# Writing the turned blocks of 16 of the 32 groups of up rows from ScalarE's DMA queue instead of SyncE's, in a two-layer decoder trunk

## The chip, the cores and the metric

The kernel runs on one core of a Trainium2 chip. The metric is the device time of one launch in microseconds (us). Three runs of the kernel before took 2085.42, 2086.52 and 2086.86 us; their median is 2086.52 us.

## What is computed

Two decoder layers on 256 tokens of width 2048, all in float32. Layer 0 mixes tokens with forgetting attention (16 heads of 128), layer 1 with a mixture of three dilated windows (8 heads). Each mixer and each MLP adds to the residual stream `x`. The change touches the MLPs alone:

```python
def sq_relu_mlp(h, w_up, w_down):
    a = jax.nn.relu(h @ w_up)
    return (a * a) @ w_down

def reference(...):
    for i in range(DEPTH):
        ...
        h = rms_norm(x, mlp_norm_g[i])
        x = x + sq_relu_mlp(h, mlp_w_up[i], mlp_w_down[i]).astype(x.dtype)
    return x
```

Here `w_up` is 2048 x 8192 and `w_down` 8192 x 2048, in each of the two layers.

## The kernel before, in words

**Products.** TensorE multiplies in a rounded 32-bit format, so every weight block is cut in two: ScalarE casts it to `hi` (L403) and VectorE subtracts that from the loaded block to give `lo` (L409). Three products (hi by hi, lo by hi, hi by lo) make one exact enough product. A weight block is 256 rows of 512 columns; SyncE loads it into one of seven `raw` buffers (L396), to which each MLP adds one more (`mlp_raw`). There are four `hi` and four `lo` buffers, and each MLP adds one `hi` (`mlp_hi`). A block in the plain form takes twelve matmuls of 512 columns (L456 to L458). In the "halved" form (`parts`, with the L471 matmuls) VectorE first makes sums of quarters of the block (L490, L495, L497), in a second `raw` buffer, and TensorE then needs 21 matmuls of 256 columns, about seven eighths of the plain work, from two pairs of `hi` and `lo`.

**The MLP.** It runs in four periods of 2048 hidden columns. Period b makes four groups of up rows of 512 columns each ("ups"). From the second period on they run mixed with the four "downs" of the period before, block by block, in the order that a table of letters U and D gives. What an up gives is needed by the downs of the next period.

**The end of an up** (`up_end`, L1214). ScalarE reads the banks and applies the relu (L1232) into `z`; VectorE transposes `z` in squares of 32 by 32 into `turned` (L1235, the tile `mlp_tr`, three buffers); four DMAs write `turned` to a buffer in DRAM so that the squares come to stand in order (`moved_blocks`, L570, the tile `blocks`, four buffers; each DMA moves 128 KB); one DMA of 512 KB reads it back into `z` (L575); ScalarE squares it (L1243) and copies it to `aT` (L1248), the stationary operand of the downs.

**The order.** All work is first recorded as operations with an engine, an assumed duration, and what they read and write (`add`). `Plan.order` then runs a list schedule over the engines PE, ACT, DVE, POOL and one "dma" line that stands for SyncE's queue, with due times worked back from the products, and the program is emitted in the order of the planned starts. So each engine, and SyncE's queue, has one fixed order; an instruction whose semaphore has not come holds up everything behind it on its engine. SyncE issues the weight loads, the block writes and the read-backs in that one order.

**Names in the rows.** `raw`, `mlp_raw`: loaded weights. `hi`, `mlp_hi`, `lo`: the cuts. `mlp_z` and `mlp_sums`: rooms for rows ahead of the transposition. `blocks`: the DRAM buffer.

Of the kernel before, what the change touches and what calls it, by code (L numbers as in the profile page):

```python
# [20 lines left out]
NT = S // P  # L21
NC = 512
# [13 lines left out]
PERIODS = DFF // D  # L36
# [12 lines left out]
LAST_HALVED = [[[], [], [4, 5, 6, 7], []], [[], [6, 7], [4, 5, 6, 7]]]  # L49
# [9 lines left out]
ROWS_BY_DMA = {"fox": (), "dil": ()}  # L59
UP_BY_DMA = [[(), (0, 1, 2, 3), (), ()], [(), (0, 1, 2, 3), (), ()]]  # L60
SHARED = 2
N_W = {"fox": 4, "dil": 3}
TURNED = {"fox": "DDDE", "dil": "DDDE"}
ROUNDS = 4
# [9 lines left out]
EARLY_NORM = 0.0  # L74
EARLY_HEADS = 0.0
EARLY_ROWS = 0.0
# [191 lines left out]
def trunk(ctx: ExitStack, tc, x, fox_w_in, fox_b_f, fox_q_gain, fox_k_gain, fox_w_out, dil_w_in,  # L268
          dil_q_gain, dil_k_gain, dil_w_out, mix_norm_g, mlp_norm_g, mlp_w_up, mlp_w_down, out):
    nc = tc.nc  # L270
    plan = Plan(["fox", "mlp0", "dil", "mlp1"])
    add = plan.add
    T = {}

    def v(item):
        return T[item.slot if isinstance(item, Item) else item]
# [35 lines left out]
    for ph in ("mlp0", "mlp1"):  # L312
        rings[ph] = dict(sigma=ring("sigma", 4, 2 * 4 * 2 * P, ph), tr=ring("tr", N_TR, NT * NC, ph),
                         z=ring("z", N_Z, 4 * S, ph), c=ring("c", N_C, 4 * S, ph), sums=ring("sums", 1, NT * NC, ph))
# [247 lines left out]
        return [[(room, x) for x in names] for names in (("12", "11"), ("22", "21"))]  # L562


    def moved_blocks(turned, into, early=0.0):

        blocks = blocks_ring.take()
        for i in range(4):
            def go(i=i):
                nc.sync.dma_start(v(blocks)[:, :, i, :].rearrange("j c y -> c j y"),  # L570
                                  v(turned)[32 * i:32 * i + 32, 0:NT * NC].rearrange("c (j y) -> c j y", j=4))
            add("dma", 0.4, go, reads=[turned], writes=[(blocks, i)])

        def back():
            nc.sync.dma_start(v(into)[:, 0:NT * NC], v(blocks).rearrange("j c i y -> (j c) (i y)"))  # L575
        add("dma", moved(512), back, reads=[(blocks, i) for i in range(4)], writes=[into], early=early)
        return [into]
# [22 lines left out]
    def normed(l, n, col, phase, source, sigmas):  # L600

        own = rings[phase]
        turned, back = (own["w"].take(), own["w"].take()) if phase == "fox" else (own["tr"].take(), own["z"].take())
        add("dve", 1.4, lambda: nc.vector.transpose(
            v(turned).rearrange("p (j t b r) -> p t b j r", t=NT, j=4, b=4),
            v(f"x{n}").rearrange("p (t b j c) -> p t b j c", t=NT, j=4, c=32)), reads=x_keys(n), writes=[turned])
        here = moved_blocks(turned, back, EARLY_NORM)
# [331 lines left out]
    for n in range(NX):  # L939
# [5 lines left out]
        for pr in range(2):  # L945
# [12 lines left out]
            for i in range(2):  # L958
                b = 2 * pr + i
# [27 lines left out]
        reads=[wf, (wfs, 0)], writes=[(wfs, 1)])  # L987
# [223 lines left out]
    out_proj(oT, fox_w_out[0], then1, "fox", sigma_o)  # L1211


    def up_end(l, phase, source, halved, by_dma, room, summed=None, rows_by_dma=False):  # L1214
        own = rings[phase]

        def end(banks):
# [7 lines left out]
            else:  # L1225
                c = own["c"].take()
# [9 lines left out]
                v(turned).rearrange("p (j t b r) -> p t b j r", t=NT, j=4, b=4),  # L1236
                v(z)[:, 0:2 * NC].rearrange("p (t b j c) -> p t b j c", t=NT, j=4, c=32)),
                reads=[(z, t) for t in range(NT)], writes=[turned, z])
            here = moved_blocks(turned, z, EARLY_ROWS)

            for t in range(NT):
                def squared(t=t):
# [21 lines left out]
    def mlp(l, layer, phase, source, sigmas, then, last=None):  # L1264
        more_weights(phase, MORE)
        downs = []
        turn = 0
        for b in range(PERIODS):
            a, a_sums = Source(), {}
            ups = []  # L1270

            def sum_of(n):
                a_sums[n] = rings[phase]["sigma"].take()
                return a_sums[n]
            for n in range(4):
                halved = HALVED[layer][b][n]
                banks = (AC if halved else AC[:2]) if b or n % 2 == 0 else BE if halved else BE[:2]
                ups.append(Unit(source, mlp_w_up[layer], 0, [(b * D + n * NC, NC)], banks,
                                up_end(l, phase, a, halved, LOW_BY_DMA and n < 3, "z" if b or n % 2 == 0 else "sums",
                                       (lambda n=n: sum_of(n)) if b == PERIODS - 1 and any(j // 2 == n for x in LAST_HALVED[layer] for j in x) else None, n in UP_BY_DMA[layer][b]),  # L1280
                                halved, sigmas, UP_ADDING[layer][b][n]))
            if b == 0:
                paired(ups[0], ups[1])
                ups[2].blocks(NP)
                ups[3].blocks(NP)
            else:
                for u, d in zip(ups, downs):
                    for c in UU_D[layer][b - 1]:
                        (u if c == "U" else d).block()
            downs = []  # L1290
            for n in range(NX):
                banks = ("E0", "E1") if turn % 2 == 0 else ("B0", "B1")
                turn += 1
                here = LAST_HALVED[layer][n] if b == PERIODS - 1 and n < len(LAST_HALVED[layer]) else ()
                if b == PERIODS - 1:
                    banks = rows_of_banks(LAST_BANKS[layer][n])
                end = quarters_to_x(n, then, here, rings[phase]["c"]) if here else add_to_x(n, then) if b == PERIODS - 1 else add_to_x(n, None, rings[phase]["sums"] if BY_DMA else None)
                downs.append(Unit(a, mlp_w_down[layer], b * D, [(n * NC, NC)], banks, end, here, a_sums, ADDING if b < PERIODS - 1 else ()))
        if last is None:
            paired(downs[0], downs[1])  # L1300
            downs[2].blocks(NP)
            downs[3].blocks(NP)
        else:
            paired(downs[0], downs[1])
            downs[2].blocks(NP)
            last(downs[3])
        fewer_weights(phase)
# [207 lines left out]
```

## Time and profile before

| what | value |
|---|---|
| median of 3 runs | 2086.52 us (2085.42 to 2086.86) |
| the profiled execution | 2085.53 us |
| its span, from the first to the last instruction | 2083.7 us |
| PE busy | 2078.4 us, 12118 matmuls |
| VectorE (DVE) busy | 1882.1 us |
| ScalarE (ACT) busy | 1472.0 us |
| GpSimd (POOL) busy | 116.1 us |
| granted TensorE clock | 1.000 |
| bytes moved by DMA | 528.57 MB, mean 254 GB/s |

How to read it: the span lies 1.8 us under the time of its own execution, and that execution is one run among those of the first row. Busy times are unions of an engine's instructions. The instructions that issue a DMA, or wait for a semaphore, are not counted as busy, so ScalarE's 1472.0 us hold none of the work that this change gives to it. In the rows of the timeline the columns are the start in us from the span's start, the duration in us, engine, line, operation, what is written and read, shapes and count; in brackets stands how long the engine was idle just before and what ended that.

### The profile page before, as it was taken

To read this page: it belongs to the slowest core of one execution; us is meant where nothing else is said; L and a number is where in the kernel's file an instruction comes from. 1 tells how busy PE (TensorE), PEld (TensorE's weight loads), DVE (VectorE), ACT (ScalarE), POOL (GpSimd) and SP (SyncE) were. 2 spreads that over 40 slices of the span, in tenths; PEclk is the share of its full clock that TensorE was granted. 3 is DMA by queue.
4 is the path that set the end of the run, shared out by engine and by line. 5 is a ranking of instruction groups with operands and counts; after the bars stand their busy time and mean duration, and the time that the engine had idled before them with its cause. 6 is when DMAs were issued, how large, how long until landed. Compare 5 with 4: busy or idle time off the path is not lost.

```text
span 2083.7 us, 33916 instructions
## 1 busy us (share of the span) xinstructions
PE 2078.4 (100%) x12118; PEld 1889.3 (91%) x12118; DVE 1882.1 (90%) x2612; ACT 1472.0 (71%) x2151; POOL 116.1 (6%) x115
## 2 busy tenths in 40 slices
PE   9999999999999999999999999999999999999999
PEld 8899888899999999998888999888999999999988
DVE  8999899999989999988799999777999999999987
ACT  7778767677677676776677777656776777676664
POOL 1100100000010000000010000100000000000000
PEclk9999999999999999999999999999999999999999
DMA  8688968698897798797877778868798888897894
GB/s 277 204 243 259 279 197 265 222 290 277 242 302 253 252 273 260 251 294 249 268 232 247 234 218 271 255 203 265 238 284 259 263 278 247 272 281 227 254 301 159
DMA packets 341467, 528.57 MB, mean 254 GB/s; under 512 B 52072, under 2 KB 145072, under 8 KB 341296
## 3 DMA queue, kind: packets, MB, share of 16 engines
q1 hardware_dynamic: 330784, 497.94, 72.7%
q0 software_dynamic: 10240, 28.32, 7.5%
q8 instruction: 95, 1.56, 0.3%
q14 instruction: 76, 0.62, 0.1%
q10 hardware_dynamic: 272, 0.13, 0.0%
HBM read 458.80 MB, written 39.19 MB: 239 GB/s over the span
## 4 chain that ended last, share of the span: by engine, by line
PE 100%; POOL 0%; DVE 0%; issue 0%; POOLq 0%
PE bank_C L471 14%; PE bank_A L471 14%; PE bank_B L456 11%; PE bank_B L458 11%; PE bank_B L457 11%; PE bank_E L471 10%; PE bank_E L456 6%; PE bank_E L457 6%; PE bank_E L458 6%; PE bank_A L456 3%; PE bank_A L458 3%; PE bank_A L457 3%; PE bank_C L847 1%; PE bank_C L892 1%; PE bank_C L845 0%; PE bank_B L471 0%
## 5 line engine op out<-in xcount | busy, mean ns | idle before, releaser
L403 ACT CAST hi<-raw 128x1024 fp32r<-128x1024 f32 (+2 forms) x808 | 802.1, 1003 | 406.2 <-PE bank_B L458 112.6
L409 DVE TENSOR_TENSOR lo<-raw,hi 128x1024 fp32r<-128x1024 f32 (+2 forms) x808 | 925.5, 1161 | 113.0 <-ACT hi L403 67.4
L457 PE MATMUL bank_B<-lo,aT 128*128 128x512 f32 x576 | 218.3, 379 | 0.0
L471 PE MATMUL bank_C<-hi,hT 128*128 128x256 f32 (+1 forms) x782 | 207.2, 302 | 0.0
L456 PE MATMUL bank_B<-hi,aT 128*128 128x512 f32 x500 | 189.7, 379 | 0.0
L458 PE MATMUL bank_B<-hi,aT 128*128 128x512 f32 x500 | 189.5, 379 | 0.0
L457 PE MATMUL bank_E<-lo,aT 128*128 128x512 f32 x480 | 181.9, 379 | 0.0
L471 PE MATMUL bank_A<-hi,mlp_sigma 128*128 128x256 f32 x880 | 171.6, 275 | 0.0
L457 PE MATMUL bank_B<-lo,hT 128*128 128x512 f32 x448 | 169.8, 379 | 0.0
L456 PE MATMUL bank_B<-hi,hT 128*128 128x512 f32 x436 | 166.3, 381 | 0.0
L458 PE MATMUL bank_B<-hi,hT 128*128 128x512 f32 x436 | 165.2, 379 | 0.0
L403 ACT CAST mlp_hi<-raw 128x1024 fp32r<-128x1024 f32 (+1 forms) x123 | 122.3, 995 | 58.1 <-PE bank_E L458 22.0
L471 PE MATMUL bank_E<-hi,hT 128*128 128x512 f32 (+1 forms) x556 | 163.0, 355 | 0.0
L471 PEld LDWEIGHTS bank_C<-hi,hT 128*128 128x128 f32 x782 | 148.1, 191 | 4.5
L409 DVE TENSOR_TENSOR lo<-raw,mlp_hi 128x1024 fp32r<-128x1024 f32 (+1 forms) x123 | 141.4, 1150 | 10.6 <-issue 2.4
L471 PE MATMUL bank_C<-lo,hT 128*128 128x256 f32 (+1 forms) x495 | 150.7, 305 | 0.0
L471 PEld LDWEIGHTS bank_A<-hi,mlp_sigma 128*128 128x128 f32 x880 | 145.5, 192 | 0.0
L471 PE MATMUL bank_A<-lo,mlp_sigma 128*128 128x256 f32 x521 | 143.3, 275 | 0.0
L456 PE MATMUL bank_E<-hi,aT 128*128 128x512 f32 x356 | 135.0, 379 | 0.0
L458 PE MATMUL bank_E<-hi,aT 128*128 128x512 f32 x356 | 134.9, 379 | 0.0
L490 DVE TENSOR_TENSOR raw<-raw 128x512 f32<-128x512 f32 x172 | 116.9, 684 | 10.3 <-DMA raw<-in_mlp_w_up_dram 10.2
L457 PEld LDWEIGHTS bank_B<-lo,aT 128*128 128x128 f32 x576 | 109.0, 189 | 14.0
(453 smaller groups left out, 4896.3 us busy)
## 6 DMA issues: line engine op xcount, KB each, us to landing
raw<-in_mlp_w_down_dram SPq DMA_DIRECT2D x224, 512.0 KB, 5.7
raw<-in_mlp_w_up_dram SPq DMA_DIRECT2D x223, 512.0 KB, 5.5
raw<-in_dil_w_in_dram SPq DMA_DIRECT2D x192, 256.0 KB, 4.5
raw<-in_fox_w_in_dram SPq DMA_DIRECT2D x94, 512.0 KB, 5.2
blocks<-mlp_tr SPq DMA_DIRECT2D x176, 128.0 KB, 4.2
mlp_z<-blocks SPq DMA_DIRECT2D x40, 512.0 KB, 6.2
mlp_raw<-in_mlp_w_up_dram SPq DMA_DIRECT2D x33, 512.0 KB, 5.5
raw<-in_fox_w_out_dram SPq DMA_DIRECT2D x32, 512.0 KB, 4.3
```

The lines of the kernel that those rows point to most:

```text
L403: add("act", on_act(n), lambda: nc.scalar.copy(r(hi)[:, 0:n], v(src)[:, at:at + n]), reads=keys, writes=[hi])
L409: add("dve", on_dve(n), lambda: nc.vector.tensor_sub(r(lo)[:, 0:n], v(src)[:, at:at + n], v(hi)[:, 0:n]), reads=[*keys, hi], writes=[lo])
L456: nc.tensor.matmul(acc, a, h, start=first and i == 0, stop=False)
L457: nc.tensor.matmul(acc, a, l, start=False, stop=False)
L458: nc.tensor.matmul(acc, b, h, start=False, stop=last and i == 1)
L471: nc.tensor.matmul(to if part is None else to[:, part * S:(part + 1) * S], stationary, moving, start=first, stop=last)
L490: add("dve", on_dve(2 * q), lambda: nc.vector.tensor_add(v(sums)[:, 0:2 * q].rearrange("p (g n) -> p g n", g=2), v(raw)[:, q:3 * q].rearra ...
L847: nc.tensor.matmul(ps[:, P:3 * P], r(a)[:, own], in_turn(r(b)[:, both], P // 2), start=opens and x == 0, stop=x == 2)
L892: nc.tensor.matmul(acc[:, 0:S], r(w)[:, c:c + P], in_turn(r(q), P), start=first, stop=False)
```

## The change

A table `UP_BY_ACT` names ups by layer, period and number. It names all four ups of the second and the third period of both MLPs, 16 of the 32. For these the four block writes leave SyncE's order: ScalarE issues them, one behind the other, as a single operation of the plan, which reads `turned` and so follows the transposition. In the plan it takes 4 x 0.43 us of ScalarE's time, and a second operation without an instruction stands for the transfer. A second table for the norms, `NORM_BY_ACT`, is empty. The read-backs stay on SyncE. Nothing is computed otherwise.

```diff
+UP_BY_ACT = [[(), (0, 1, 2, 3), (0, 1, 2, 3), ()]] * 2
+NORM_BY_ACT = ()
...
-    def moved_blocks(turned, into, early=0.0):
+    def moved_blocks(turned, into, early=0.0, by_act=False):
         blocks = blocks_ring.take()
-        for i in range(4):
+        if by_act:
+            def there():
+                for i in range(4):
+                    nc.scalar.dma_start(v(blocks)[:, :, i, :].rearrange("j c y -> c j y"),
+                                        v(turned)[32 * i:32 * i + 32, 0:NT * NC].rearrange("c (j y) -> c j y", j=4))
+            all_four = [(blocks, i) for i in range(4)]
+            add("act", 4 * Plan.ISSUE, there, reads=[turned, *all_four])
+            add("dma", 1.6, None, reads=[turned], writes=all_four).soon = 0.8
+        for i in () if by_act else range(4):
             def go(i=i):
                 nc.sync.dma_start(v(blocks)[:, :, i, :].rearrange("j c y -> c j y"),
...
-            here = moved_blocks(turned, z, EARLY_ROWS)
+            here = moved_blocks(turned, z, EARLY_ROWS, turned_by_act)
```

The plan is made anew from the changed operations. PE's order and GpSimd's come out row for row as they were. On ScalarE, VectorE and SyncE the order differs in places. In the rows below the lines of the change are two higher than before up to L567 and ten higher from there on (L403 is L405, L570 is L580 or, for ScalarE, L573).

ScalarE in the second period of the first MLP, at the end of its first up, before (this is the stretch from 490 to 499 us of the profile):

```order
L1232 ACTIVATE mlp0_z0_3077<-mlp0_z0_3077,rstd1_75 128x512
L403 CAST hi1_128<-raw4_124 128x768
L403 CAST hi2_129<-raw5_125 128x1024
L403 CAST hi3_130<-raw6_126 128x1024
L403 CAST mlp0_hi0_3081<-raw0_120 128x768
L403 CAST hi0_127<-raw1_121 128x1024
```

The same place with the change:

```order
L1242 ACTIVATE mlp0_z0_3077<-mlp0_z0_3077,rstd1_75 128x512
L405 CAST hi1_128<-raw4_124 128x768
L405 CAST hi2_129<-raw5_125 128x1024
L573 DMA blocks0_143<-mlp0_tr2_3076 32x4x256 x4
L405 CAST hi3_130<-raw6_126 128x1024
L405 CAST mlp0_hi0_3081<-raw0_120 128x768
L405 CAST hi0_127<-raw1_121 128x1024
```

The four DMAs stand behind the second cast that follows the relu, and five casts of weights stand right behind them.

SyncE at the same end of an up, before:

```order
L570 DMA blocks0_143<-mlp0_tr2_3076 32x4x256 x4
L396 DMA raw4_124<-in_mlp_w_down_dram 128x2x512
L396 DMA raw5_125<-in_mlp_w_up_dram 128x2x512
L396 DMA raw0_120<-in_mlp_w_up_dram 128x2x512
L575 DMA mlp0_z0_3077<-blocks0_143 128x1024
L396 DMA mlp0_raw0_3080<-in_mlp_w_down_dram 128x2x512
```

With the change:

```order
L398 DMA raw4_124<-in_mlp_w_down_dram 128x2x512
L398 DMA raw5_125<-in_mlp_w_up_dram 128x2x512
L398 DMA raw0_120<-in_mlp_w_up_dram 128x2x512
L585 DMA mlp0_z0_3077<-blocks0_143 128x1024
L398 DMA mlp0_raw0_3080<-in_mlp_w_down_dram 128x2x512
L398 DMA raw2_122<-in_mlp_w_down_dram 128x2x512
```

The block writes are gone, and the read-back stands behind the same three loads as before.

VectorE at the end of the last up of the second period of the second MLP, before (from 1688 to 1696 us):

```order
L409 TENSOR_TENSOR lo2_133<-raw0_120,hi0_127 128x1024
L409 TENSOR_TENSOR lo3_134<-raw1_121,mlp1_hi0_12317 128x1024
L490 TENSOR_TENSOR raw4_124<-raw3_123 128x512
L409 TENSOR_TENSOR lo0_131<-raw2_122,hi1_128 128x1024
L495 TENSOR_TENSOR raw4_124<-raw4_124,raw3_123 128x256
L1235 STREAM_TRANSPOSE mlp1_tr2_12312<-mlp1_z0_12313 128x8x4x32
```

With the change:

```order
L411 TENSOR_TENSOR lo2_133<-raw0_120,hi0_127 128x1024
L1245 STREAM_TRANSPOSE mlp1_tr2_12312<-mlp1_z0_12313 128x8x4x32
L411 TENSOR_TENSOR lo3_134<-raw1_121,mlp1_hi0_12317 128x1024
L411 TENSOR_TENSOR lo0_131<-raw2_122,hi1_128 128x1024
L492 TENSOR_TENSOR raw4_124<-raw3_123 128x512
L411 TENSOR_TENSOR lo1_132<-raw3_123,hi2_129 128x768
```

The transposition has moved ahead of two cuts and two sums, to right behind the cut that it followed at a distance.

More of the change, by code (lines that the diff above doesn't have):

```diff
@@ L606, in normed @@
             v(f"x{n}").rearrange("p (t b j c) -> p t b j c", t=NT, j=4, c=32)), reads=x_keys(n), writes=[turned])
-        here = moved_blocks(turned, back, EARLY_NORM)
+        here = moved_blocks(turned, back, EARLY_NORM, l in NORM_BY_ACT)
         for b in range(4):
@@ L1211, in trunk, with up_end @@
     out_proj(oT, fox_w_out[0], then1, "fox", sigma_o)
-    def up_end(l, phase, source, halved, by_dma, room, summed=None, rows_by_dma=False):
+    def up_end(l, phase, source, halved, by_dma, room, summed=None, rows_by_dma=False, turned_by_act=False):
         own = rings[phase]
@@ L1279, in mlp @@
                                 up_end(l, phase, a, halved, LOW_BY_DMA and n < 3, "z" if b or n % 2 == 0 else "sums",
-                                       (lambda n=n: sum_of(n)) if b == PERIODS - 1 and any(j // 2 == n for x in LAST_HALVED[layer] for j in x) else None, n in UP_BY_DMA[layer][b]),
+                                       (lambda n=n: sum_of(n)) if b == PERIODS - 1 and any(j // 2 == n for x in LAST_HALVED[layer] for j in x) else None, n in UP_BY_DMA[layer][b], n in UP_BY_ACT[layer][b]),
                                 halved, sigmas, UP_ADDING[layer][b][n]))
```

## The prediction, made before the changed kernel was run

> **What bounds the kernel now.** I read the page's busy times and its chain first, then the waits of PE, then PE's own rows, and last the four stretches in which the change acts.
>
> ```profile
> PE 2078.4 (100%) x12118; PEld 1889.3 (91%) x12118; DVE 1882.1 (90%) x2612; ACT 1472.0 (71%) x2151; POOL 116.1 (6%) x115
> ...
> PE 100%; POOL 0%; DVE 0%; issue 0%; POOLq 0%
> ```
>
> The chain that ended last is PE alone. A busy PE need not be a PE at its rate, since the ends of matmuls are modelled. So the next two views look for waits and at the distance from start to start.
>
> ```profile
> PE bank_C L908 <- POOL ident masks.py:199: 1.7, 1, 1.7
> ```
>
> That is the whole list of PE's waits (over 0.15 us): one, of 1.7 us, at the start of the program.
>
> ```profile
> 1734.24 0.38 PE L456 MATMUL bank_B<-hi,aT 128*128 128x512 f32 x1
> 1734.45 0.38 PE L457 MATMUL bank_B<-lo,aT 128*128 128x512 f32 x1
> 1734.67 0.38 PE L458 MATMUL bank_B<-hi,aT 128*128 128x512 f32 x1
> ```
>
> Matmuls of 512 columns start 0.21 to 0.22 us apart although each is drawn 0.38 long: they run one behind the other. The changed places lie in four stretches, the second and third period of each MLP (columns: length, busy time and count of PE, weight loads, DVE, ACT, POOL, then granted clock, DMA share, GB/s):
>
> ```profile
> 455.00:620.00 165.00, 165.00 (x1052) 152.72 (x1051) 149.46 (x195) 120.46 (x146) 15.43 (x16) 1.00 0.91 277
> 620.00:775.00 155.00, 155.00 (x983) 143.28 (x982) 145.40 (x194) 110.16 (x135) 6.00 (x7) 1.00 0.83 258
> 1535.00:1697.00 162.00, 162.00 (x1050) 150.45 (x1049) 150.74 (x201) 117.28 (x141) 14.55 (x15) 1.00 0.90 272
> 1697.00:1850.00 153.00, 153.00 (x987) 141.93 (x986) 145.91 (x198) 110.61 (x136) 6.03 (x7) 1.00 0.83 259
> ```
>
> PE is busy without a gap in all four, at full clock. VectorE has 6 to 9% left, ScalarE 27 to 29%, and the DMA engines 9 to 17%. The matmuls and their order stay the same. So time can be **lost** (an operand comes too late for PE) but hardly won: outside PE's busy time the span has 2083.7 - 2078.4 = 5.3 us, 1.7 of them the wait above.
>
> **What the change takes from SyncE.** It takes 16 x 4 = 64 issues.
>
> ```profile
> L570 SPq DMA_DIRECT2D blocks<-mlp_tr x176: 303/436/2006, 326.7 to 2009.9; - x176
> ...
> DMA to landing us min/median/max: 2.0/3.8/8.5
> ```
>
> At the median of 0.436 us these are 28 us of SyncE's time. With them go about half of the waits for the transposition, the first row here:
>
> ```profile
> SPq L570 <- DVE mlp_tr L1235: 52.9, 27, 4.5
> SPq L396 <- DVE lo L409: 844.4, 455, 7.3
> ```
>
> The second row says what that is worth. SyncE spends 844 us waiting for a cut to free a `raw` buffer; more free time on it makes most loads no earlier. The cover for the rest is PE's zero wait. I put the gain at **0**; its bounds are 0 and 5.3 us.
>
> **What it gives to ScalarE.** Four issues at 16 places. The nearest row is ScalarE's only issue of its own, at the end of the program:
>
> ```profile
> L1466 ACTq DMA_DIRECT2D out_dram<-x x1: 412/412/412, 2080.6 to 2080.6; - x1
> ```
>
> 4 x 0.412 = 1.65; SyncE's median gives 4 x 0.436 = 1.74. I take **1.7 us per place**, 27 us in all. The lower bound is nothing (the sequencer may issue while the engine still works on the cast ahead). The upper bound is the slowest group of four among these places:
>
> ```profile
> 697.64 4.24 SPq L570 DMA_DIRECT2D blocks<-mlp_tr  x4
> ```
>
> Behind the issues stand casts, and behind those VectorE's subtractions and PE. Of the places that I followed, the first is the tightest. Its rows (ACT, DVE, then the matmul that first reads the fourth of the four `lo`):
>
> ```profile
> 493.53 1.05 ACT L403 CAST hi<-raw 128x1024 fp32r<-128x1024 f32 x1 [0.18 <-PE bank_C L471]
> 494.86 1.05 ACT L403 CAST hi<-raw 128x1024 fp32r<-128x1024 f32 x1 [0.28 <-PE bank_C L471]
> ...
> 492.17 1.25 DVE L1235 STREAM_TRANSPOSE mlp_tr<-mlp_z 128x1024 f32<-128x1024 f32 x1
> 493.34 4.32 DVE L409 TENSOR_TENSOR lo<-raw,hi 128x1024 fp32r<-128x1024 f32 x4
> ...
> 499.52 0.38 PE L457 MATMUL bank_B<-lo,aT 128*128 128x512 f32 x1
> ...
> L409 DVE TENSOR_TENSOR lo<-raw,hi 128x1024 fp32r<-128x1024 f32 (+2 forms) x808 | 925.5, 1161 | 113.0 <-ACT hi L403 67.4
> ```
>
> The transposition ends at 493.42, ScalarE's cast ahead of the issues at 494.58: no wait is added. Issues to 494.58 + 1.70 = 496.28, the next cast (1.05) to 497.33, its subtraction (1.16) to 498.49; PE reads it at 499.52. **1.0 us is left**, where 1.9 were (497.66 to 499.52). At 2.7 us per place nothing is left, at 4.24 PE waits 1.5 us here.
>
> Elsewhere there is more room. At 696 ScalarE stands idle behind the issues' place:
>
> ```profile
> 694.66 0.58 ACT L713 COPY mlp_sums<-bank_B 128x512 f32<-128x512 f32 x1
> 698.89 1.05 ACT L403 CAST mlp_hi<-raw 128x1024 fp32r<-128x1024 f32 x1 [3.64 <-PE bank_E L458]
> 696.38 1.23 DVE L1235 STREAM_TRANSPOSE mlp_tr<-mlp_z 128x1024 f32<-128x1024 f32 x1
> ```
>
> Here the issues do wait for VectorE, from 695.24 to 697.61, and end at 699.3. The casts behind come 0.4 us late. Eleven of the 16 transpositions end before ScalarE gets there. The first is the one above at 493, the last this one, through at 1845.31 while ScalarE's cast ends at 1846.75:
>
> ```profile
> 1844.07 1.24 DVE L1235 STREAM_TRANSPOSE mlp_tr<-mlp_z 128x1024 f32<-128x1024 f32 x1
> 1845.70 1.05 ACT L403 CAST mlp_hi<-raw 128x1024 fp32r<-128x1024 f32 x1
> ```
>
> Five end after, by 1.2 to 3.6 us. The 3.6 stand here:
>
> ```profile
> 1689.39 0.72 ACT L1232 ACTIVATE mlp_z<-mlp_z,rstd 128x512 f32<-128x512 f32 x1
> 1690.02 1.04 ACT L403 CAST hi<-raw 128x1024 fp32r<-128x1024 f32 x1
> 1695.05 1.05 ACT L403 CAST hi<-raw 128x1024 fp32r<-128x1024 f32 x1 [2.83 <-DVE raw L497]
> 1693.40 1.24 DVE L1235 STREAM_TRANSPOSE mlp_tr<-mlp_z 128x1024 f32<-128x1024 f32 x1
> ```
>
> In the new order this transposition stands four instructions earlier. It can start when the relu is through, at 1690.11, and end at 1691.35, 0.3 us after ScalarE's cast at 1691.06; the issues then end at 1693.1, and the one short cast that stood there still ends before 1695.05, up to which ScalarE was idle. I price ScalarE's part at **0**: the cover is the lead of the cuts.
>
> **What it does to the read-back.** It stays on SyncE and now waits for writes that ScalarE issues. At 493 these start 1.1 us later than SyncE's did (494.58 for 493.44) and, being together, end 0.7 us later.
>
> ```profile
> 493.44 2.11 SPq L570 DMA_DIRECT2D blocks<-mlp_tr  x4
> 499.14 0.75 SPq L575 DMA_DIRECT2D mlp_z<-blocks  x1
> ```
>
> They land about 496.28 + 3.8 = 500.1: SyncE may stand 0.9 us at the read-back, with weight loads queued behind it. One row shows what a late load costs PE:
>
> ```profile
> 660.48 0.69 DVE L490 TENSOR_TENSOR raw<-raw 128x512 f32<-128x512 f32 x1 [2.59 <-DMA raw<-in_mlp_w_up_dram]
> ```
>
> VectorE stood 2.59 us waiting for a load, and PE's list of waits has nothing there. So 0.9 us is covered: **0**. The rows that are read back feed the downs of the next period.
>
> **The sum.** 0 + 0 + 0 on the profiled execution's 2085.53 us (span 2083.7 and 1.8 around it). That run lies 1.0 us under the median of 2086.52; I put the forecast on the median: **2086.5 us**.
>
> A rule of the Trainium skill speaks against the change: Perfetto Trace Analysis, section DMA Instruction — HWDGE (DVE, Sync), says that the profiled window of such an instruction holds a wait for the exclusive use of the descriptor generator. If ScalarE and SyncE shared one, each of the four issues could wait for one load's issue of SyncE. No run here shows the two at once; the first rival is that mechanism.
>
> **The rivals.**
> 1. *ScalarE's issues are slow, because SyncE issues loads at the same time.*
>
> ```profile
> L396 SPq DMA_DIRECT2D raw<-in_mlp_w_up_dram x223: 367/368/1610, 344.0 to 1974.1; - x112
> ```
>
> With one such issue waited for each time, a place takes 4 x (0.436 + 0.368) = 3.2 us; with the slowest group it takes 4.24. The subtraction above, made at all 16 places with the two transpositions at 1694 and 1737 at their earlier rows, gives PE about 1 us of waiting in all at 3.2 and about 4 at 4.2: 2087.5 to 2090.5. At 5 us (the slowest group, and two loads waited for) eight places fall short, 10 us in all: **2096.4, slower**. It decides from 2.7 us per place on and passes 0.2% (4.2 us) at about 4.2. For it: DMA share 0.83 to 0.91 in these stretches. Against it: the median of 0.436, with such loads all around.
>
> 2. *SyncE stands at the read-back.* Where ScalarE gets to its issues late, the writes land late, and all loads behind the read-back with them. The cover is the 2.59 us above and the 1.0 us left at the tightest place. If SyncE stood 4.6 us, 1 us more than that, at half of the places, PE would wait 8 x 1 = 8 us: **2094.5, slower**. Against it: 0.9 us worked out above, and three loads that stand ahead of the read-back.
>
> 3. *SyncE's freedom brings time.* At most 5.3 us: 2081.2. Nothing in PE's rows asks for it.
>
> 4. *The change does not do what it says.* In the order ScalarE has 16 groups of four and SyncE 64 rows fewer; no chance.
>
> **How the numbers follow.** Forecast at 2086.5: 0.76. First rival in its mild form (up to 2090.5, within 0.2%): 0.11. Its hard form: 0.06. Second rival: 0.05. Third: 0.02. So slower 0.11, same 0.87, faster 0.02; 0.2%, 4.2 us, is about what a measurement of this kernel can tell from no change. The range goes from 2085.0, 0.4 us under the lowest run, to 2090.5, the end of the mild form.
>
> **What would show it.** Right: PE's list of waits still has one entry, ScalarE's four issues take 1.6 to 2.5 us a place and stand in what were gaps, and SyncE's waits for L1235 are about halved. Wrong by the first rival: ScalarE's issues of over 0.8 us each, and PE or VectorE waiting for `hi` behind them. Wrong by the second: a long wait of SyncE at the read-back, then casts waiting for `raw`. The forecast falls if PE shows waits in the four stretches that sum to over 4 us.

## The result, and the profile after

The changed kernel takes **2089.95 us** (median of 20 runs, 2088.65 to 2092.97) against 2086.84 for the kernel before beside it (20 runs, 2085.41 to 2089.48). The ratio is 1.0015 with a 95% interval of 1.0009 to 1.0022: 3.1 us slower, within 0.2%, but not the time of before. The profiled execution has a span of 2088.3 us, 4.6 more than before.

Busy times and chain of the changed kernel, from its page. Lines up to L567 are two higher than before, later ones ten: ScalarE's block writes are L573, SyncE's L580, the read-back L585.

```profile
PE 2078.7 (100%) x12118; PEld 1888.8 (90%) x12118; DVE 1882.4 (90%) x2612; ACT 1469.4 (70%) x2151; POOL 116.3 (6%) x115
...
PE 98%; DVE 1%; DMA 1%; issue 0%; SPq 0%; ACT 0%; DVEq 0%
```

PE's busy time is what it was (2078.4), VectorE's too. So nothing became longer work: the time is waiting, and the chain now has VectorE and a DMA in it. PE's waits (engine, tile and line, whom it waited for, us, times, the longest):

```profile
PE bank_A L473 <- DVE lo L411: 3.3, 3, 1.6
PE bank_C L918 <- POOL ident masks.py:199: 1.7, 1, 1.7
PE bank_A L458 <- ACT hT L973: 0.8, 1, 0.8
PE bank_A L459 <- DVE lo L411: 0.2, 1, 0.2
```

The first row is new and is the loss. The other three lie within the first 20 us of the program, ahead of every changed place; the 1.7 us stood there before too, and the other two leave PE's later rows only 0.2 us behind those of before. The 3.3 us are three waits, found among PE's rows (start, length, and in brackets the idle time ahead with its releaser):

```profile
731.62 0.38 PE L473 MATMUL bank_A<-lo,mlp_sigma 128*128 128x256 f32 x1 [1.56 <-DVE lo L411]
...
1850.64 0.38 PE L473 MATMUL bank_A<-lo,mlp_sigma 128*128 128x256 f32 x1 [0.36 <-DVE lo L411]
1859.85 0.38 PE L473 MATMUL bank_A<-lo,mlp_sigma 128*128 128x256 f32 x1 [1.42 <-DVE lo L411]
```

All three are in or just behind a **third** period. The stretches of the prediction say the same (columns as there):

```profile
455.00:620.00 165.00, 165.00 (x1053) 152.74 (x1052) 152.45 (x199) 120.45 (x147) 15.40 (x16) 1.00 0.91 279
620.00:775.00 155.00, 153.44 (x966) 141.50 (x965) 141.97 (x190) 108.77 (x134) 5.99 (x7) 1.00 0.81 254
1535.00:1697.00 162.00, 162.00 (x1051) 150.45 (x1050) 150.34 (x199) 115.50 (x141) 14.55 (x15) 1.00 0.91 270
1697.00:1850.00 153.00, 153.00 (x980) 141.75 (x979) 144.53 (x197) 110.70 (x136) 6.03 (x7) 1.00 0.84 260
```

Both second periods have PE busy to the last 0.01 us. The first MLP's third period lost 1.56, and what the second's lost came just past its end, from 1850 on. Set one by one against the same rows of before, PE's matmuls start 0.2 us later up to 725, 2.1 from 735 on, 2.2 from 1750 on and 4.5 from 1865 on. So the loss stands at these waits and hardly anywhere else, but it is 4.3 us in this execution and not 3.3: each matmul is drawn longer than the distance to the next, and that hides a part of every wait.

ScalarE's issues were not alike. The line of all 64 (min, median, max in ns), the widest of the quick groups, and four long groups (a row is a group end to end):

```profile
L573 ACTq DMA_DIRECT2D blocks<-mlp_tr x64: 309/459/1904, 493.8 to 1852.7; - x64
...
657.17 2.58 ACTq L573 DMA_DIRECT2D blocks<-mlp_tr  x4
697.01 4.59 ACTq L573 DMA_DIRECT2D blocks<-mlp_tr  x4
774.45 4.91 ACTq L573 DMA_DIRECT2D blocks<-mlp_tr  x4
1810.55 4.59 ACTq L573 DMA_DIRECT2D blocks<-mlp_tr  x4
1849.51 4.18 ACTq L573 DMA_DIRECT2D blocks<-mlp_tr  x4
```

The median of 0.459 is what was priced. But added up, twelve groups took 1.4 to 2.5 us and these four 4.1 to 4.8. GpSimd's rows name a companion of each: the transfer that adds a down onto x, 512 KB long.

```profile
652.61 0.86 POOL L681 DMA_DIRECT2D x<-mlp_sums  x1 [43.21 <-ACT mlp_sums L723]
695.77 0.86 POOL L681 DMA_DIRECT2D x<-mlp_sums  x1 [42.30 <-ACT mlp_sums L723]
...
1808.39 0.88 POOL L681 DMA_DIRECT2D x<-mlp_sums  x1 [42.24 <-DVE lo L411]
1846.37 0.86 POOL L681 DMA_DIRECT2D x<-mlp_sums  x1 [4.71 <-ACT mlp_sums L723]
```

The slow groups begin 1.2, 1.2 (behind one at 773.27), 2.2 and 3.1 us behind such an issue. At 652.61 it is 4.6 us to the next group, and that group was quick. SyncE's loads are no such companion: beside the group at 697 SyncE issues at 695.25 and then not before 704.05.

What came behind the group at 697, on ScalarE and then VectorE:

```profile
701.72 1.05 ACT L405 CAST hi<-mlp_raw 128x1024 fp32r<-128x1024 f32 x1 [6.25 <-PE bank_C L473]
...
702.80 1.22 DVE L411 TENSOR_TENSOR lo<-mlp_raw,hi 128x1024 fp32r<-128x1024 f32 x1 [2.77 <-ACT hi L405]
```

The cast starts at 701.72, where a cast stood at 698.89 before (PE was 0.2 us late there already), and VectorE stands 2.77 us for it. PE feels that only at 731.62, 29 us on. In 690 to 740 us VectorE has hardly any slack to make up with; before and after:

```profile
690.00:740.00 50.00, 50.00 (x317) 46.19 (x317) 47.96 (x64) 33.40 (x42) 1.71 (x2) 1.00 0.82 253
```

```profile
690.00:740.00 50.00, 48.44 (x304) 44.54 (x304) 44.98 (x60) 32.13 (x40) 1.71 (x2) 1.00 0.77 237
```

Before, VectorE was busy for 47.96 of these 50 us, so it makes up little of what it loses. And the first loss brings a second: at 717.86 it stands 1.52 us for a load, ahead of PE's wait.

```profile
717.86 0.69 DVE L492 TENSOR_TENSOR raw<-raw 128x512 f32<-128x512 f32 x1 [1.52 <-DMA raw<-in_mlp_w_up_dram]
```

The same delay can also cost nothing. The longest group, 4.91 us at 774, made VectorE wait 2.22 us in the same way, and PE's next wait comes only at 1850:

```profile
780.32 0.96 DVE L411 TENSOR_TENSOR lo<-raw,hi 128x768 fp32r<-128x768 f32 x1 [2.22 <-ACT hi L405]
```

In the second MLP VectorE stood for ScalarE's casts right behind both slow groups, 1.88 and 1.46 us, and for loads 1.09 us at 1832.28 and 0.42 at 1856.37:

```profile
1816.31 1.23 DVE L411 TENSOR_TENSOR lo<-raw,mlp_hi 128x1024 fp32r<-128x1024 f32 x1 [1.88 <-ACT mlp_hi L405]
...
1854.65 0.96 DVE L411 TENSOR_TENSOR lo<-raw,hi 128x768 fp32r<-128x768 f32 x1 [1.46 <-ACT hi L405]
```

SyncE's waits answer as forecast: those for the transposition halved (52.9 before), and those for the cuts took the time over (844.4 before).

```profile
SPq L398 <- DVE lo L411: 896.6, 469, 8.4
...
SPq L580 <- DVE mlp_tr L1245: 26.2, 14, 4.5
SPq L585 <- DMA blocks<-mlp_tr: 24.2, 21, 4.2
```

### The profile page after: what moved, and what is told of

The parts are those of the page before. It is cut to its first block, busy times and chain, and to the rows that moved or that the text cites. A ratio compares the mean times of both kernels' runs of the same rounds, so it can differ in the third digit from the quotient of the medians.

```text
span 2088.3 us, 33901 instructions
## 1 busy us (share of the span) xinstructions
PE 2078.7 (100%) x12118; PEld 1888.8 (90%) x12118; DVE 1882.4 (90%) x2612; ACT 1469.4 (70%) x2151; POOL 116.3 (6%) x115
## 3 DMA queue, kind: packets, MB, share of 16 engines
q8 instruction: 95, 1.56, 0.3%
## 4 chain that ended last, share of the span: by engine, by line
PE 98%; DVE 1%; DMA 1%; issue 0%; SPq 0%; ACT 0%; DVEq 0%
PE bank_C L473 14%; PE bank_A L473 13%; PE bank_B L458 10%; PE bank_B L460 10%; PE bank_B L459 10%; PE bank_E L473 10%; PE bank_E L458 6%; PE bank_E L460 6%; PE bank_E L459 6%; PE bank_A L459 3%; PE bank_A L460 3%; PE bank_A L458 3%; PE bank_C L857 1%; DVE lo L411 1%; PE bank_C L902 1%; PE bank_C L855 0%
## 5 line engine op out<-in xcount | busy, mean ns | idle before, releaser
L405 ACT CAST hi<-raw 128x1024 fp32r<-128x1024 f32 (+2 forms) x808 | 801.5, 1003 | 415.0 <-PE bank_B L460 106.9
L405 ACT CAST mlp_hi<-raw 128x1024 fp32r<-128x1024 f32 (+1 forms) x123 | 122.2, 994 | 59.5 <-PE bank_C L473 12.1
```

Source lines behind the costliest of these rows:

```text
L405: add("act", on_act(n), lambda: nc.scalar.copy(r(hi)[:, 0:n], v(src)[:, at:at + n]), reads=keys, writes=[hi])
```

## The experiments

Two theories went in. **Slow issues**: ScalarE's issues take its time, four groups too much of it. **New order**: the plan, made anew from other operations, puts VectorE's work or the loads in a worse order, whoever issues. All runs but those that say so have 11 timed runs, beside 27 to 33 of the kernel before. The ratio on record need not be the quotient of the two medians (in e3 1.0003, where the medians give 1.0007), and its interval reaches some 1.9 us either way. So where it holds 1.0000 (e1, e2, e3, e15, e16), the reading rests on PE's waits and not on the time.

### Engine and order apart: e1, e2

e1 keeps the changed kernel's order, SyncE issues:

```diff
-                    nc.scalar.dma_start(v(blocks)[:, :, i, :].rearrange("j c y -> c j y"),
+                    nc.sync.dma_start(v(blocks)[:, :, i, :].rearrange("j c y -> c j y"),
```

> The order of the changed plan on every engine, but the 64 block writes are issued by SyncE at the places where the changed kernel has ScalarE issue them. Slow-issue theory (ScalarE is held by its own issues, above all the four groups that took 4.2 to 4.9 us): no loss, 2086.8 us and no wait of PE over 0.15 us in the four stretches. New-order theory (the plan's new order on VectorE, with transpositions ahead of cuts that PE needs sooner): the loss stays, 2089.5 to 2090.5 us, with PE waiting near 730 and 1858.

e2 keeps the order of before, ScalarE issues the 64 writes:

```diff
-                nc.sync.dma_start(v(blocks)[:, :, i, :].rearrange("j c y -> c j y"),
+                (nc.scalar if by_act else nc.sync).dma_start(v(blocks)[:, :, i, :].rearrange("j c y -> c j y"),
```

> The order of before on PE, VectorE and GpSimd, but the 64 block writes are issued by ScalarE, where the old plan puts each single write. Slow-issue theory: a loss as large as the change's or larger, 2089 to 2094 us, since the old plan kept no time on ScalarE for them; the slow groups show up again, at the places where SyncE's were slow before (698, 772, 1845). New-order theory: 2086.8 us.

Measured: e1 2088.3 us, ratio 1.0007 (0.9998 to 1.0016); e2 2088.14, 1.0009 (1.0000 to 1.0018). By the medians each has about half of the loss (e2 less than the slow-issue theory expected), and PE's waits tell the places. In e2 PE waits at 731 us as in the changed kernel; its next largest wait, at 1858, is of 0.49:

```profile
731.63 0.38 PE L472 MATMUL bank_A<-lo,mlp_sigma 128*128 128x256 f32 x1 [1.67 <-DVE lo L410]
```

In e1 that wait is gone, but those past 1849 are there:

```profile
1849.36 0.38 PE L473 MATMUL bank_A<-lo,mlp_sigma 128*128 128x256 f32 x1 [0.34 <-DVE lo L411]
1858.10 0.38 PE L473 MATMUL bank_A<-lo,mlp_sigma 128*128 128x256 f32 x1 [0.95 <-DVE lo L411]
```

So neither theory is enough alone: the wait at 731 follows ScalarE's issues, and past 1849 the new order makes PE wait 1.3 us without one issue of ScalarE.

### The slow places apart: e3, e4

e3 leaves the four slow places to SyncE, e4 gives ScalarE these four alone:

```diff
-UP_BY_ACT = [[(), (0, 1, 2, 3), (0, 1, 2, 3), ()]] * 2
+UP_BY_ACT = [[(), (0, 1, 2, 3), (0, 2), ()], [(), (0, 1, 2, 3), (0, 1), ()]]
```

> ScalarE issues twelve of the 16 groups; the four that were slow (near 697, 774, 1810 and 1849) stay on SyncE. Slow-issue theory: the twelve take 1.4 to 2.6 us each, no loss, 2086.8 us, PE without waits. A loss by the plain sum of ScalarE's issue time would be three quarters of it, 2089.1 us. New-order theory: between the two kernels, 2087 to 2090 us.

```diff
-UP_BY_ACT = [[(), (0, 1, 2, 3), (0, 1, 2, 3), ()]] * 2
+UP_BY_ACT = [[(), (), (1, 3), ()], [(), (), (2, 3), ()]]
```

> ScalarE issues only the four groups that were slow in the change. Slow-issue theory: nearly the whole loss, 2089 to 2090 us, issues of 3 to 5 us a group and VectorE waiting for hi behind them. Plain-sum theory: a quarter of the loss, 2087.6 us.

Measured: e3 2088.02, ratio 1.0003 (0.9994 to 1.0012), ScalarE's groups all 1.5 to 2.4 us; e4 2089.43, 1.0012 (1.0003 to 1.0021), groups of 2.4 to 4.3. e3 has one wait, of 1.07 us at 1858.23. e1 has one there too, without ScalarE's issues, so the twelve quick groups show no cost of their own. e4's time came as the slow-issue theory expected, but not for its reason: of its 2.6 us of waits only 0.59 at 731.21 and 0.22 at 1851.47 stand behind the slow places. The other two, 0.52 at 673.23 and 1.26 at 1669.47, stand ahead of any group on ScalarE in their MLP, and what made them was not followed. So e4 does not show that the four groups are nearly the whole loss.

### What makes an issue slow: e9

e9 leaves GpSimd's adding transfers out of the changed kernel:

```diff
-                added(lambda: v(f"x{n}"), lambda: v(sums), [(sums, t) for t in range(NT)], x_keys(n), 2.55)
+                add("dma", 2.55, None, reads=[(sums, t) for t in range(NT)], writes=x_keys(n))
```

> This kernel is the changed one in which GpSimd's accumulating transfers of the first three periods (x<-mlp_sums, 512 KB each) are left out, so that the downs of these periods are not added to x; the plan still counts them, and the order of all engines is the changed kernel's. Theory that GpSimd's accumulating transfer in flight is what stretches ScalarE's issues: the four groups at about 697, 774, 1811 and 1850 us fall from 4.1 to 4.8 us to 1.4 to 2.5 us like the other twelve, PE's stall at 731 goes, the one at 1859 shrinks to at most 1.1 us (what the run with SyncE's issues in the new order had), and the time comes 1.5 to 3 us down, to 2087 to 2088.5 us. Rival, that SyncE's loads issued at the same moment stretch them: the loads are where they were, the four groups stay at 4 us and more, the stalls and the time (about 2089.9 us) stay.

The groups at the four places, without GpSimd's transfers:

```profile
697.18 2.24 ACTq L573 DMA_DIRECT2D blocks<-mlp_tr  x4
...
772.79 1.86 ACTq L573 DMA_DIRECT2D blocks<-mlp_tr  x4
...
1813.48 2.18 ACTq L573 DMA_DIRECT2D blocks<-mlp_tr  x4
...
1849.80 2.34 ACTq L573 DMA_DIRECT2D blocks<-mlp_tr  x4
```

All four are quick, and the wait at 731 is gone. So it is GpSimd's transfer that stretches these groups. (A single issue can be stretched without it: one of e9's, at 1652.80, took 1.60 us.) e7 below shows the same from the other side. Its order puts the transfer 7.9 us ahead of the group at 698 and 2.3 us ahead of the one at 735, and now the second is slow:

```profile
698.11 2.47 ACTq L573 DMA_DIRECT2D blocks<-mlp_tr  x4
735.62 4.46 ACTq L573 DMA_DIRECT2D blocks<-mlp_tr  x4
```

The expectation of the **time** failed: 2090.16 us, ratio 1.0016 (1.0007 to 1.0025). Another wait had come in the second MLP, where VectorE stood for a load:

```profile
1676.39 0.69 DVE L492 TENSOR_TENSOR raw<-raw 128x512 f32<-128x512 f32 x1 [6.48 <-DMA raw<-in_mlp_w_up_dram]
```

The load landed 13.7 us behind its issue; why so late was not followed. PE waited 2.27 us behind it. Past 1850 PE waited another 1.1 us in e9, with all of ScalarE's groups there quick. So a load that lands late can cost PE's time without a slow group.

### By period and by MLP: e5, e6, e16, e12

e5 has the change in the second periods alone, e6 in the third, e16 in the first MLP, e12 in the second:

```diff
+UP_BY_ACT = [[(), (0, 1, 2, 3), (), ()]] * 2
...
+UP_BY_ACT = [[(), (), (0, 1, 2, 3), ()]] * 2
...
+UP_BY_ACT = [[(), (0, 1, 2, 3), (0, 1, 2, 3), ()], [(), (), (), ()]]
...
+UP_BY_ACT = [[(), (), (), ()], [(), (0, 1, 2, 3), (0, 1, 2, 3), ()]]
```

> The change in the second period of each MLP alone. If ScalarE's slow groups of the third period are what costs time: eight groups of 1.4 to 2.5 us, no stall of PE at 731 us, and a time of 2086.5 to 2087.3 us, the kernel before's. If any group of issues on ScalarE costs PE time, or the mere freedom of SyncE shifts work badly, about half of the 3.1 us is left here: 2088.2 us or more.

> The change in the third period of each MLP alone. If ScalarE's slow groups of the third period are what costs time: four groups of over 4 us, PE's stalls at about 731 us (1.7 us) and 1850 to 1860 us (1 to 2 us), and 2089 to 2090.5 us, the changed kernel's time. If the loss is spread over both periods: 2088.2 us or less, with half of the stalls.

> The change in the first MLP alone. If the two MLPs' losses stand apart: a stall of 1.5 to 2 us at 731 us, none at 1850 to 1860 us, and 2087.5 to 2089 us. If they depend on one another: no stall at 731 us, or stalls at 1850 to 1860 us too.

> The change in the second MLP alone. If the loss has two parts, the slow group at 697 us in the first MLP and late loads of raw in the second: no stall at 731 us, VectorE waiting 1.5 us or more for a load of raw at about 1830 us, stalls of PE of 1.1 to 2.1 us between 1849 and 1860 us, and 2087.5 to 2089 us. If the second MLP's stalls are only carried on from the first: none, and the time of before.

Measured: second periods 2085.86, ratio 0.9997 (0.9988 to 1.0005), no wait of PE; third periods 2088.5, 1.0010 (1.0002 to 1.0019); first MLP 2087.9, 1.0006 (0.9997 to 1.0015); second MLP 2089.56, 1.0016 (1.0007 to 1.0025). The second periods cost nothing. e6 met its expectation in part: two of its groups took over 4 us, not four, and PE waited at 734.16 (1.68 us) but not past 1850. Its first wait, at 691.60 (1.26 us), lies ahead of any slow group; its cause was not followed. e16 has one wait, of 1.63 us at 731.59. e12 has two, of 1.46 at 1850.29 and 1.31 at 1859.39, in sum and in time more than was expected.

The two MLPs' losses stand apart, neither carried into the other. Their sum (1.6 + 2.7 = 4.3 us) and the whole's 3.1 cannot be told apart: the two intervals reach 1.9 us either way, the whole's 1.4.

### ScalarE's time alone: e11, e15, e10

The kernel before, its writes on SyncE; at the place of 697 us ScalarE copies 384 columns of the turned tile into a spare one, four, eight or eleven times:

```diff
             def go(i=i):
+                for _ in range(HOLD if held and i == 0 else 0):
+                    nc.scalar.activation(T["hold"], v(turned)[:, 0:384], AF.Copy)
                 nc.sync.dma_start(v(blocks)[:, :, i, :].rearrange("j c y -> c j y"),
```

> The same with four copies, about 1.6 us, the length that a quick group of four issues has. If ScalarE's time at this place costs only beyond what the cuts' lead covers: no stall of PE at 731 us and the time of before, 2086 to 2087.3 us. If VectorE is so full here that each microsecond of ScalarE's is lost: a stall of about 0.5 us or more at 731 us.

> The kernel before with ScalarE held at 697 us by eight copies, 4.4 us by the 0.55 us that one took. If a hold as long as the slow group makes PE wait as in the changed kernel: a stall of 0.5 to 1.8 us between 705 and 735 us, and 2087.3 to 2089 us. If the slow group costs by something else than ScalarE's time: no stall, and the time of before.

> The kernel before, with SyncE's writes as they were; at the place of the first MLP's third period where the changed kernel's slow group stands (697 us), ScalarE makes eleven copies of 384 columns of the turned tile into a spare tile, about 4.3 us in all. If it is the length of time that ScalarE is taken at this place which makes PE wait: a stall of PE of 1.3 to 2 us at about 731 us, more than 30 us behind, none elsewhere, and 2087.5 to 2089 us. If it is the transfers (where the writes are issued, when they land) and not ScalarE's time: no stall, and the time of before.

A copy took 0.55 us, not 0.4, so the holds came out at 2.20, 4.42 and 6.08 us; e15 was added because the longest overshot. e11: 2086.27, ratio 0.9995 (0.9986 to 1.0004), no wait of PE. e15: 2088.53, 1.0008 (0.9999 to 1.0017). e10: 2089.72, 1.0015 (1.0006 to 1.0023), with PE's waits at 706 and 707 already (1.4 us in sum). The rows of e15, ScalarE, VectorE and PE in turn:

```profile
697.38 4.42 ACT L572 ACTIVATE hold<-mlp_tr 128x384 f32<-128x384 f32 x8 [2.13 <-DVE mlp_tr L1238]
...
703.71 1.23 DVE L410 TENSOR_TENSOR lo<-mlp_raw,hi 128x1024 fp32r<-128x1024 f32 x1 [2.64 <-ACT hi L404]
...
732.37 0.38 PE L472 MATMUL bank_A<-lo,mlp_sigma 128*128 128x256 f32 x1 [1.68 <-DVE lo L410]
```

Without one write on ScalarE this is the changed kernel's chain: ScalarE taken for 4.4 us, VectorE waiting 2.64 (there 2.77), PE waiting 1.68 (there 1.56; here 0.49 at 729.42 besides), 29 us later. The order is that of before, so VectorE's rows can be set one by one against the same rows there. The hold makes them 2.7 us later; 11 us on it is only 1.5, and from 15 us on 3.8. VectorE had made up some of the delay when it stood twice more for ScalarE's casts, 1.10 and 1.13 us. A group as long as a quick one (2.20) is free at the same place. So at 697 us it is ScalarE's time that costs, and between 2.2 and 4.4 us lies the point from which PE waits for it.

### The late loads: e14

e1, with the four writes and the read-back at one place (1809 us) left out:

```diff
-                for i in range(4):
+                for i in range(0 if left_out else 4):
...
         def back():
+            if left_out:
+                return
```

> The changed kernel's order with all block writes issued by SyncE, as in the first of these experiments, but at the third place of the second MLP's third period (1809 us) the four writes and the read-back are left out, so that the squares there are of rows that were not turned back. That takes 1 MB of transfers and five issues out of the stretch ahead of 1830 us; VectorE's and PE's orders are as they were. If the loads of raw that land late behind these transfers are what makes PE wait: VectorE's wait for the load at about 1830 us falls from 1.9 us to 0.7 us or less, PE's stalls at 1849 and 1858 us (0.5 and 1.1 us) fall to 0.5 us or less in sum, and the time comes to 2086 to 2087.5 us. If the new order of VectorE's work itself does it: the stalls stay at 1 us or more, and the time at 2088 us or more.

Measured: 2086.38 us, ratio 0.9999 (0.9991 to 1.0008), no wait of PE left. The cuts' sum behind the load, in e1 and then in e14:

```profile
1831.02 0.69 DVE L492 TENSOR_TENSOR raw<-raw 128x512 f32<-128x512 f32 x1 [1.89 <-DMA raw<-in_mlp_w_up_dram]
```

```profile
1828.66 0.69 DVE L493 TENSOR_TENSOR raw<-raw 128x512 f32<-128x512 f32 x1
```

VectorE's 1.89 us of waiting for the load are gone, and with them PE's 1.3. In e1 that load was issued at 1821.72, 1.2 us later than before, when PE itself stood about 1 us behind: in time, then. But SyncE's group of writes at 1809 had held the first two loads behind it by 2 to 3 us, so that they crowd with it; e1's row, where before the group took 2.59 us:

```profile
1809.22 5.16 SPq L573 DMA_DIRECT2D blocks<-mlp_tr  x4
```

And in 1817 to 1823 us SyncE's loads took longer to land (min, median, max, of those whose landing is on record), before and then e1:

```profile
DMA to landing us min/median/max: 5.2/5.3/5.4
```

```profile
DMA to landing us min/median/max: 7.0/8.4/9.8
```

So e1's waits past 1849 come of a load that lands late behind the writes and the read-back, not of the order of VectorE's work, which e14 shares with e1. Which of the two delays, the 5.16 us of issues or the 1 MB of transfers, does more is not told apart: e14 takes away both.

This is not yet the changed kernel. There SyncE issues none of these writes, and its loads in 1817 to 1823 us land in 5.4 to 8.4 us (median 5.7; before 5.3, in e1 8.4). VectorE waits there for both, the casts behind the slow groups and the loads, as its rows above show. Without a slow group of ScalarE's, PE waited 1.1 to 1.3 us past 1849 (e1, e3, e9); the changed kernel waits 1.8. No run parts the two.

### A plan that knows the price, and a version without it: e7, e13

e7 reserves ScalarE's time for a long group at every place, e13 gives ScalarE ten of the quick groups alone:

```diff
-            add("act", 4 * Plan.ISSUE, there, reads=[turned, *all_four])
+            add("act", 4.5, there, reads=[turned, *all_four])
```

> The changed kernel whose plan reserves 4.5 us of ScalarE for each group of four issues. If the stalls come of a slow group that the order does not allow for: the order puts other work of ScalarE ahead of it or gives VectorE's cuts more lead, the stall at 731 us shrinks below 1 us and the time falls to 2087 to 2088.5 us. If ScalarE's time itself is the cost, wherever it stands: the stalls stay at 3 to 4 us in sum, at other places, and the time at 2089.5 us or more.

```diff
-UP_BY_ACT = [[(), (0, 1, 2, 3), (0, 1, 2, 3), ()]] * 2
+UP_BY_ACT = [[(), (0, 1, 2, 3), (0, 2), ()], [(), (0, 1, 2, 3), (), ()]]
```

> The change without the third period of the second MLP and without the two slow places (697 and 774 us) of the first: ten groups on ScalarE, those that were quick. If the loss has the two parts named: no stall of PE beyond the start, and the time of before, 2086 to 2087.3 us. If any issues on ScalarE in a third period cost: a stall of 0.5 us or more, and 2087.5 us or more.

e7 missed: 2091.71 us (9 runs), ratio 1.0025 (1.0015 to 1.0034), with 4.8 us of PE's waits at other places. A reserve at all 16 places, where four needed it, gave an order that was worse; its waits were not followed. e13, the ten groups that the runs had found harmless, came back: 2086.11, ratio 0.9997 (0.9988 to 1.0005), but with 0.7 us of waits at 1543 and 1552, ahead of the second MLP's first group; e10 and e7 have waits at about that time too. They stand in the slowest of its 11 executions (2088.42), where PE's rows lose 2.7 us against before, nearly all in the second MLP's second period; why was not followed. No run beat the kernel before beyond its interval, as is to be expected of a kernel whose PE had no waits.

All runs, with PE's waits between 20 and 2080 us in the profiled execution, which lay up to 2.8 us above the median (e6, e9) and 1.1 below it (e10). The list leaves a part of the loss out, as above:

| kernel | median minus before, us | PE's waits, us |
|---|---|---|
| before | 0 | 0 |
| changed | +3.1 | 3.3 |
| e1 new order, SyncE issues | +1.8 | 1.3 |
| e2 old order, ScalarE issues | +1.6 | 2.3 |
| e3 twelve quick places | +1.5 | 1.1 |
| e4 four slow places | +2.9 | 2.6 |
| e5 second periods | -0.7 | 0 |
| e6 third periods | +1.9 | 3.3 |
| e7 4.5 us reserved | +5.1 | 4.8 |
| e9 no adding transfers | +3.6 | 3.7 |
| e10, e15, e11 holds of 6.1, 4.4, 2.2 us | +2.8, +2.2, -0.6 | 1.6, 2.4, 0 |
| e12 second MLP | +2.7 | 2.8 |
| e13 ten quick places | -0.8 | 0.7 |
| e14 one turn left out | +0.1 | 0 |
| e16 first MLP | +1.6 | 1.6 |

The time follows PE's waits to within about 1.5 us, less than one interval.

## Why the prediction was wrong

*PE bounds the kernel, and SyncE's freedom is worth nothing.* Right. PE's busy time did not move, and SyncE's 26.7 us less at the transposition went into waiting for the cuts.

*1.7 us per place on ScalarE.* About right at twelve places (1.4 to 2.5 us added up), wrong at four (4.1 to 4.8). **This is the step that failed: one price for all places, and the row with the other price taken as a bound.** The row of 4.24 us that was quoted as the upper bound starts at 697.64, at one of the 16 places. It was no unlucky SyncE group but the price behind GpSimd's transfer onto x, and ScalarE paid 4.59 there. That transfer and another group of its kind stood in the same trace:

```profile
695.54 0.86 POOL L671 DMA_DIRECT2D x<-mlp_sums  x1 [43.52 <-ACT mlp_sums L713]
...
1845.34 4.09 SPq L570 DMA_DIRECT2D blocks<-mlp_tr  x4
```

The price goes with the transfer and not with the place. At 1808 SyncE's group took 2.59 us before, 5.1 us behind a transfer; the new order brought the two to within 2.2 us, and the group took 4.59. Of the changed kernel's 3.3 us of waits the 1.56 at 731 are shown to come of this term (e2, e9, e15, e16).

*The place at 696: issues end at 699.3, casts 0.4 us late.* Measured 701.6 and 2.8 us, by the same mis-sized term. The prediction had counted this place among those with more room.

*The tightest place is 493, with 1.0 us left.* The end came out, by luck: the last issue ended at 496.1 (worked out 496.28), the cast behind started at 496.21, PE did not wait. But the issues began 0.8 us earlier than worked out and took 2.32 us where 1.70 were priced, and the two errors cancel. They began earlier because ScalarE's sequencer issued while the engine still worked on the cast ahead, which the prediction had kept for its lower bound:

```profile
493.76 1.05 ACT L405 CAST hi<-raw 128x1024 fp32r<-128x1024 f32 x1 [0.18 <-PE bank_C L473]
493.79 2.32 ACTq L573 DMA_DIRECT2D blocks<-mlp_tr  x4
496.21 1.05 ACT L405 CAST hi<-raw 128x1024 fp32r<-128x1024 f32 x1 [1.40 <-PE bank_C L473]
```

But the tightest place was sought in the wrong measure. The slack was taken from each place's next matmul, as if lost time ended there. VectorE, before 94% busy in the stretch of 620 to 775 and 96% in 690 to 740, carries it on and adds to it, and PE waits 29 us later (e15 shows it without the change). The room at the place was not the room that counted.

*The read-back on SyncE costs nothing.* As a wait of SyncE, right: 24.2 us for 25.7. But the loads were priced only by what stands ahead of them on SyncE, and VectorE's wait of 2.59 us at 660 was taken to show that a late load is covered. In e1, with the new order, a load issued in time landed late in the second MLP and cost PE 1.3 us (e14). The sum had no term for that. How much of the changed kernel's 1.8 us past 1849 is its part, and how much is the mis-sized issues', stays open.

*The rivals.* The first had the right form: slow groups of 4.2 us were to give about 4 us of waiting and 2087.5 to 2090.5. That the measured time lies there is luck in part, since it had counted them at all 16 places and they came at four. Its cause was wrong. SyncE issued nothing beside the group at 697, and with GpSimd's transfers gone and SyncE's loads in place the groups are quick (e9), so SyncE's loads are not it. The rule that the prediction cited, of the Trainium skill (Perfetto Trace Analysis, DMA Instruction — HWDGE (DVE, Sync)), puts a wait for the descriptor generator into the window of an issue; the runs leave such a wait at most a share of the quick groups' 1.4 to 2.5 us. The second rival is refuted as a wait of SyncE. The third asked for 5 us that nobody had.

*What would show it.* The mark that was set, waits of over 4 us in the four stretches, was too loose: 3.3 us, half of them just past the last stretch, are 3.1 us of time when PE has no slack. And 0.2% (4.2 us) is not the least that can be told from no change: with 20 runs of each the interval of the loss is 1.9 to 4.6 us.

Left open: how GpSimd's transfer stretches the issues (by its descriptors, or by filling the DMA engines); how the 1.8 us of waits past 1849 are shared between ScalarE's two slow groups and the late loads; the waits of e4 at 673 and 1669 and of e6 at 691, and the order's sensitivity that e7 shows.

## What to carry to other kernels

Price a moved step by the row that stands at its own place. Before you call an outlier a bound, read its start time and look for what else starts beside it: that neighbour may make the step slow on any engine, and a new order can move it to another place. Where an engine has only some 5% of its time left, as VectorE here, a delay does not end at the next consumer, so look for the room tens of microseconds on. Moving a DMA's issue moved its cost to another engine and did not shorten it (median 0.436 us on SyncE before, 0.459 on ScalarE).

## What the hardware showed that was not expected

An issue of 128 KB took 0.31 to 0.7 us on ScalarE as a rule, and up to 1.2 in the twelve quick groups. In the groups that began in the first 3.1 us behind GpSimd's adding transfer of 512 KB the first issue still took 0.31, the second to fourth 0.8 to 1.9. SyncE's groups were stretched alike (4.24 us for four before, 5.16 in e1). That the first is spared looks more like something that fills up than like a lock; no run settles it.

After a long wait PE's clock fell. In e9 PE waited 2.27 us up to 1678.73, the clock stayed at 1.00 up to 1680, and then came (stretch, length, PE, weight loads, VectorE, ScalarE, GpSimd, granted clock, DMA share, GB/s):

```profile
1680.00:1682.00 2.00, 2.00 (x7) 1.61 (x6) 2.00 (x4) 2.00 (x5) 0.56 (x2) 0.54 0.40 77
1682.00:1684.00 2.00, 2.00 (x8) 1.59 (x7) 1.88 (x5) 2.00 (x3) 1.69 (x3) 0.61 0.89 325
1684.00:1686.00 2.00, 2.00 (x13) 1.81 (x12) 2.00 (x4) 1.70 (x4) 0.73 (x1) 1.00 1.09 315
```

The granted clock was near half for most of 4 us, and 15 matmuls ran in them where 26 would have at the rate of the last row: 11 missing at 0.154 us are 1.7 us on top of the wait, by this estimate. In e15 the clock fell as well: behind PE's waits of 0.49 and 1.68 us, 3 us apart, it was 0.50 in the stretch of 733 to 736. A wait of 1.68 us alone (e6) left it at 1.00. The changed kernel's waits of up to 1.56 us left the clock at 1.00 in every stretch above. The Trainium skill (TensorE: Matmul & The Clock Gate, Part 1) gives about 3.4 us of idling for this; here 2.27 us were enough.
